# An mLSTM mixer's value product and output gate with features on partitions, and its head norm by products with ones

## The chip, the cores and the metric

One Trainium2 chip, one of its cores. The metric is the device time of one execution in microseconds (us). The kernel's weights, 292 MB with everything that is moved, come from the chip's memory in each execution.

## The reference

A trunk of two layers over 256 context tokens and 256 latent tokens of 1024 features. Layer 0 is a bidirectional chunkwise mLSTM mixer with 4 heads, layer 1 multi-head latent attention; behind each stands a gated convolutional feed-forward network. The change touches the mixer of layer 0. Cut to what it touches:

```python
x_m = h @ w_up                                   # 1024 -> 2048
x_c = silu(dwconv(x_m))
q, k = split(x_c @ w_qk)                         # 4 heads of 256
v = x_m @ w_v                                    # 4 heads of 512
s = chunk_scan(q, k, v, gates)                   # both directions, summed; per head: weights @ v
o = sigmoid(h @ w_og)                            # 1024 -> 2048, 4 heads of 512
hsum = o * s
y = head_rms_norm(hsum, norm_g) @ w_out          # per token and head over 512 features, eps 1e-6
```

The output is the latent stream in fp32.

## The kernel before

**Products.** Every operand is fp32 and is split in two: `hi`, a rounded copy (made by ACT), and `lo`, the rest (made by DVE, source minus `hi`). One product is three matmuls, hi x hi, hi x lo, lo x hi (`mm3`, lines 464 to 466). A tile is 128 partitions by 512 columns; sums lie in eight PSUM banks of that size.

**Weights.** `Stream` brings the weights in chunks of 128 x 1024 fp32 (512 KB) in a fixed order, `_plan`; `_stat` lays a chunk out as stationary operand (eight blocks of 128 x 128), `_mov` as moving operand (two rows of 512). SP issues the loads to `raw`, ACT casts `w` hi (lines 367 and 377), DVE subtracts `w` lo (lines 368 and 380). There are three `w` buffers, so that the cast of chunk n+3 waits until the products of chunk n have ended.

**Order.** Each engine works through its own queue in order. That order is fixed when the kernel is built: a scheduler places the instructions of all stages by its own estimate of readiness, not always as the code is written. A stage's main products are interleaved with background generators: `tick`, called once per weight chunk, advances the first generator in `bg` by one step, and the second begins when the first has ended. `drain` runs them to their end.

**The mixer's stages** (function `build`):

1. `w_up`: 16 chunks of `w_up`; with the convolution, `x_c` and sums of `x_m` go to memory.
2. `w_og`, 109 to 197 us: 16 chunks `og`, four for each head `s`. `tokmm` holds four banks, one per group `t` of 128 tokens: stationary is `hT` (tokens become partitions), moving the weights. After four chunks `evac` makes four sigmoids `o` and writes them to `od` in memory on ACT's queue (lines 883 and 884).
3. `w_v`, from 197 us: the value product, by a scheme with fewer multiplications over sums `s` of `xs`; chunks `vt2` and on, 12 matmuls each, and `vt2` chunks are also written back (`t2d`).
4. For h = 0 to 3: `w_qk(h)`, eight chunks of 24 matmuls, with `gate_chain`, `post(h - 2)` and `head(h - 1)` as background; then `av(h - 1)`, then `s_mm(h)`, the scores.
   - `head` makes the weights `W` (tokens by tokens), normalises them, and transposes the needed 128 x 128 blocks by PE into `PT[0..2]`, each split in hi and lo.
   - `v_load` and `v_steps` bring `v` and `od` back by POOL's queue (`vr`, `oh`).
   - `av` multiplies: per token group `t` stationary `PT` blocks, moving `v` of 512 features; context tokens need two blocks, latent tokens four. DVE multiplies the bank by the gate into `oh`.
   - `post` is the head norm over the 512 features, which lie along the free axis: ACT squares with a running sum into `ss` (128 x 1 each), square root, reciprocal 128 x 4 on DVE, four multiplications by a scalar per partition; later 16 transposes `hnT` on PE, and from their banks the split `hn` (hi on ACT at line 1248, lo on DVE at line 1249, both with the norm's weight `mng` as a scalar per partition). `hn[k]`, k = 4h + e, has features on partitions.
5. The output product "mout", context tokens first: 16 chunks of 12 matmuls of 512 columns (`outmm`; chunk k needs `hn[k]`, stationary). Under chunks 0 to 7 run `head(3)` and `post(2)`; then `av(3)`; under 8 to 11 `post(3)`; then 12 to 15. Under them also runs the modulation of the later stages (`junk<-ar,bc` on DVE). Then 16 chunks for the latent tokens, with the layer norm of the context tokens as background.

## Time and profile before

| | |
|---|---|
| three runs | 1343.89, 1345.22, 1345.07 us; median 1345.07 |
| the profiled execution | 1345.53 us, of which the span 1343.8 |
| granted clock of the PE array | 0.999 |
| PE, DVE, ACT, POOL busy | 99%, 80%, 53%, 9% of the span |
| matmul records | 6671 |
| memory read and written | 260.28 MB and 30.58 MB |

PE is TensorE's array, PEld its weight loads (they overlap), DVE VectorE, ACT ScalarE, POOL GpSimd, SP SyncE. A row of the timeline reads: start in us, length in us, engine, line, operation, output<-inputs, shapes, count, and in brackets how long the engine sat idle before it and what ended the wait. A row of the groups reads: line, engine, operation, output<-inputs, count | busy us, mean ns of one | idle us ahead of it and what ended most of it. The queue of an engine is written with a q (ACTq, POOLq, SPq): these rows are DMA issues.

### The profile page before, as it was taken

What the parts mean: (1) busy time and instruction counts of PE and PEld (TensorE: products, weight loads), DVE (VectorE), ACT (ScalarE), POOL (GpSimd) and SP (SyncE); (2) the same over time, 40 slices, a digit from 0 to 9 for tenths busy, and PEclk for the clock granted to TensorE, in tenths of its full rate; (3) what the DMA queues carried; (4) which work ended last, traced back from release to release, by engine and by line L of the source; (5) the groups of instructions that cost most, each with busy time, mean ns of one, the idle gap of its engine ahead of it and who ended that gap; (6) DMA issues with size and microseconds to landing.
All of it is one profiled execution on the core that took longest, in us unless ns stands there. A gap on an engine that the chain in (4) does not pass through costs nothing.

```text
span 1343.8 us, 18757 instructions
## 1 busy us (share of the span) xinstructions
PE 1333.9 (99%) x6671; PEld 1121.2 (83%) x6671; DVE 1072.5 (80%) x1774; ACT 708.1 (53%) x1240; POOL 123.1 (9%) x216
## 2 busy tenths in 40 slices
PE   9999999999999999999999999999999999999997
PEld 6877888888888888888898888888888988988886
DVE  5798766687888697787889878778787898898884
ACT  4675443445644545374643334333468767677661
POOL 0122000011011010210002000001100011000100
PEclk9999999999999999999999999999999999999999
DMA  9889748789765374666737777675877424476760
GB/s 375 298 292 342 227 172 256 233 281 309 251 212 196 110 240 133 224 215 211 245 107 257 235 241 238 225 245 165 233 264 244 127 82 162 150 219 194 266 188 32
DMA packets 88093, 292.09 MB, mean 217 GB/s; under 512 B 11640, under 2 KB 12152, under 8 KB 88000
## 3 DMA queue, kind: packets, MB, share of 16 engines
q1 hardware_dynamic: 61696, 215.75, 48.7%
q0 software_dynamic: 17520, 57.70, 13.8%
q10 hardware_dynamic: 8784, 17.45, 3.5%
q8 instruction: 52, 0.85, 0.3%
q14 instruction: 41, 0.34, 0.1%
HBM read 260.28 MB, written 30.58 MB: 216 GB/s over the span
## 4 chain that ended last, share of the span: by engine, by line
PE 95%; DMA 2%; DVE 1%; ACT 1%; issue 0%; DVEq 0%; ACTq 0%
PE fin L1602 8%; PE tok L464 6%; PE fin L465 6%; PE fin L466 6%; PE fin L464 6%; PE tok L466 6%; PE tok L465 6%; PE y L1686 5%; PE qk L466 4%; PE qk L464 4%; PE qk L465 4%; PE y L465 4%; PE y L466 4%; PE y L464 4%; PE up L747 2%; PE up L464 1%
## 5 line engine op out<-in xcount | busy, mean ns | idle before, releaser
L380 DVE TENSOR_TENSOR w<-raw,w 128x1024 fp32r<-128x1024 f32 (+1 forms) x256 | 307.7, 1205 | 112.0 <-ACT w L377 110.9
L377 ACT CAST w<-raw 128x1024 fp32r<-128x1024 f32 (+1 forms) x256 | 265.3, 1038 | 240.6 <-PE tok L466 83.7
L601 DVE SCALAR_TENSOR_TENSOR junk<-ar,bc 128x1024 f32<-128x1024 f32 x128 | 155.8, 1217 | 4.4 <-ACT mod L616 2.7
L465 PE MATMUL fin<-h,w 128*128 128x512 f32 (+1 forms) x376 | 141.2, 376 | 0.0
L464 PE MATMUL fin<-h,w 128*128 128x512 f32 (+1 forms) x376 | 141.2, 376 | 0.0
L466 PE MATMUL fin<-h,w 128*128 128x512 f32 (+1 forms) x376 | 141.1, 375 | 0.0
L1602 PE MATMUL fin<-h,w 128*128 128x256 f32 (+1 forms) x624 | 108.7, 337 | 0.0
L1602 PEld LDWEIGHTS fin<-h,w 128*128 128x128 f32 x624 | 95.9, 190 | 12.5
L464 PE MATMUL qk<-xc,w 128*128 128x512 f32 x256 | 100.4, 392 | 0.0
L466 PE MATMUL qk<-xc,w 128*128 128x512 f32 x256 | 99.7, 390 | 0.0
L465 PE MATMUL qk<-xc,w 128*128 128x512 f32 x256 | 99.6, 389 | 0.0
L465 PEld LDWEIGHTS fin<-h,w 128*128 128x128 f32 x376 | 70.8, 188 | 13.0
L464 PEld LDWEIGHTS fin<-h,w 128*128 128x128 f32 x376 | 70.7, 188 | 13.0
L466 PEld LDWEIGHTS fin<-h,w 128*128 128x128 f32 x376 | 70.8, 188 | 12.6
L466 PEld LDWEIGHTS qk<-xc,w 128*128 128x128 f32 x256 | 48.0, 188 | 10.1
L465 PEld LDWEIGHTS qk<-xc,w 128*128 128x128 f32 x256 | 48.1, 188 | 9.8
L464 PEld LDWEIGHTS qk<-xc,w 128*128 128x128 f32 x256 | 48.1, 188 | 9.7
L784 ACT ACTIVATE fg<-fg 128x512 f32<-128x512 f32 (+1 forms) x44 | 23.1, 526 | 57.0 <-DVE fg L782 50.8
L464 PE MATMUL tok<-w,hT 128*128 128x512 f32 x128 | 49.9, 390 | 0.0
L466 PE MATMUL tok<-w,hT 128*128 128x512 f32 x128 | 49.8, 389 | 0.0
L465 PE MATMUL tok<-w,hT 128*128 128x512 f32 x128 | 49.8, 389 | 0.0
L1686 PE MATMUL y<-w,fz 128*128 128x512 f32 x198 | 47.2, 394 | 0.3 <-DVE w L380 0.2
(492 smaller groups left out, 3138.4 us busy)
## 6 DMA issues: line engine op xcount, KB each, us to landing
raw<-in_ws SPq DMA_DIRECT2D x281, 512.0 KB, 4.7
ar<-in_adaT SPq DMA_DIRECT2D x80, 512.0 KB, 4.8
raw<-in_ws POOLq DMA_DIRECT2D x13, 512.0 KB, 7.2
raw<-in_ws SPq DMA_DIRECT2D x12, 384.0 KB, 6.2
adaw<-in_adaf SPq DMA_DIRECT2D x8, 512.0 KB, 6.2
xmd<-xr POOLq DMA_DIRECT2D x16, 256.0 KB, 4.7
xcd<-cv POOLq DMA_DIRECT2D x16, 256.0 KB, 4.8
xs<-xmd POOLq DMA_DIRECT2D x16, 256.0 KB, 5.6
```

The lines of the kernel that those rows point to most:

```text
L377: k.nc.scalar.copy(h[:, :cols], src)
L380: k.nc.vector.tensor_sub(l[:, :cols], src, h[:, :cols])
L464: mm(out, w[0], x[0], start=start, stop=False)
L465: mm(out, w[0], x[1], start=False, stop=False)
L466: mm(out, w[1], x[0], start=False, stop=stop)
L601: nc.vector.scalar_tensor_tensor(o, w, 1.0, self.bc[j], op0=ALU.mult, op1=ALU.mult, accum_out=col[:, k, j:j + 1])
L747: nc.tensor.matmul(ps[m], w[f][:, wi, m * 128:(m + 1) * 128], self.hT[f][:, hi], start=done[0] == 1, stop=done[0] == 24)
L784: nc.scalar.activation(tmp[:, :n], tmp[:, :n], AF.Silu)
L1602: nc.tensor.matmul(ps[:, :m], w[x][:, k * 128:(k + 1) * 128], hT(k)[:, :m], start=k == 0 and x == j, stop=k == 7 and x != j, skip_group_ch ...
L1686: nc.tensor.matmul(ps[b], a[:, p, ts], w[q][:, cs], start=j == 0 and n == 0 and not more, stop=j == end and n == 2, skip_group_check=True)
```

## The change

- The output gate is made with weights stationary and `hT` moving: each of the 16 chunks gives one bank of 128 features by 512 tokens, and each bank has its sigmoid and its write at once. The chunks' number and size and the number of matmuls stay.
- `head` groups the transposed blocks by the source block: `PT[0]` and `PT[1]` hold all four token groups of source 0 and 1, `PT[2]` those of sources 2 and 3 for the two latent groups.
- `av` has `v` stationary and `PT` moving. For each group `e` of 128 features: six matmuls of 512 tokens and six of the 256 latent tokens. Its result has features on partitions, so that nothing has to be transposed.
- `post` sums over partitions: ACT squares the four `oh`, DVE adds them, the sum is split, and two products with a matrix of ones (`ones`, 128 x 128) leave the sum over all 512 features in each partition of a bank `rms`. Then a square root and a reciprocal over the whole 128 x 512, and per `e` one operation (`oh` times `mng` times `rms`) and a split into `hn`. One `yield` more stands between the products with ones and the rest.
- Head 3 is normed in two halves: `av(3)` multiplies by the gate for tokens 0 to 255 and 256 to 511 apart; `post` of the first half is background of output chunks 8 to 11, of the second half of chunks 12 to 15, and each is drained behind them.

Counts: PE loses 64 transposes, has 96 matmuls of 512 and 96 of 256 columns in `av` for 144 of 512, and gains six of 512 and four of 256 with ones. DVE loses four reciprocals of 128 x 4 and 16 multiplications by a scalar, and reads 16 times fewer from PSUM for `hn`; it gains additions, reciprocals of 128 x 512 (three) and 128 x 256 (two), and the products with `rms`. POOL and SP keep their number of instructions.

```diff
@@ _plan, _pack
-    for s in range(4):
-        for c in range(4):
-            add(("og", s, c), 1024)
+    for m in range(16):
+        add(("og", m, 0), 1024)
...
-            b = _mov(i["m_w_og"][0][:, a * 512:(a + 1) * 512], 2 * c, 2)
+            b = _stat(i["m_w_og"][0], a, 0, 8)
@@ w_og
+        for m in range(16):
+            w = st.use(("og", m, 0))
+            ps = self.ps("tok")
+            for k in range(8):
+                c = slice(k * 128, (k + 1) * 128)
+                self.mm3(ps, (w[0][:, c], w[1][:, c]), (self.hT[k][:, 0], self.hT[k][:, 1]), k == 0, k == 7)
             self.tick(1, ADA_T)
+            if m == 1:
+                self.gates()
             o = self.s2("o")
+            nc.scalar.activation(o, ps, AF.Sigmoid)
+            nc.scalar.dma_start(self.od[m // 4, m % 4], o)
@@ head
+        for grp in ([(t, 0) for t in range(4)], [(t, 1) for t in range(4)], [(t, s) for s in (2, 3) for t in (2, 3)]):
@@ av
+        for e in range(4):
             ps = self.ps("av")
+            es = slice(e * 128, (e + 1) * 128)
+            for s in range(4):
+                x = PT[s] if s < 2 else PT[2][:, :, (s - 2) * 256:(s - 1) * 256]
+                o = ps if s < 2 else ps[:, 256:512]
+                for n, (i, j) in enumerate(((0, 0), (0, 1), (1, 0))):
+                    nc.tensor.matmul(o, v[s][:, i, es], x[:, j], start=s == 0 and n == 0, stop=s == 3 and n == 2,
+                                     skip_group_check=True)
@@ post
+        for e in range(4):
+            q = self.s2("sq")
+            nc.scalar.activation(q[:, c], tt[e][:, c], AF.Square)
+            if e:
+                nc.vector.tensor_tensor(sq[0][:, c], sq[0][:, c], q[:, c], op=ALU.add)
+            sq.append(q)
+        u = self.u("sq")
+        self.split(u[:, 0, c], u[:, 1, c], sq[0][:, c])
         yield
         if h < 2:
             yield
+        ps = self.ps("rms")
+        for x in range(2):
+            nc.tensor.matmul(ps[:, c], self.ones, u[:, x, c], start=x == 0, stop=x == 1)
+        r = self.s2("rms")
+        nc.scalar.activation(r[:, c], ps[:, c], AF.Sqrt, bias=self.keps, scale=1.0 / 512.0)
+        nc.vector.reciprocal(r[:, c], r[:, c])
+        yield
...
+            nc.vector.scalar_tensor_tensor(tt[e][:, c], tt[e][:, c], g[:, k:k + 1], r[:, c], op0=ALU.mult, op1=ALU.mult)
+            self.split(u[:, 0, c], u[:, 1, c], tt[e][:, c])
@@ build
-        tt = k.av(3)
-        k.bg = [k.post(3, tt)]
+        halves = slice(0, 256), slice(256, 512)
+        tt = k.av(3, halves)
+        k.bg = [k.post(3, tt, halves[0])]
         k.outmm("mout", range(8, 12), hn, pc, 0, 16, 1)
         k.drain()
+        k.bg = [k.post(3, tt, halves[1])]
...
         k.outmm("mout", range(12, 16), hn, pc, 0, 16, 1, n2=ADA_M)
+        k.drain()
```

**Where instructions stand.** ACT's queue at the end of the output gate, before. `L377 CAST w` with a `t2d` write behind it is the first value chunk, the two later casts of `w` the second and third; `o<-tok` are the last four sigmoids.

```order
L377 CAST w<-raw 128x1024
L379 DMA t2d<-raw 128x1024
L469 CAST s_1806<-xs_1636 128x512
L377 CAST w<-raw 128x1024
L469 CAST s_1811<-xs_1637 128x256
L469 CAST s_1811<-xs_1730 128x256
L883 ACTIVATE o<-tok 128x512
L884 DMA od<-o 128x512
L883 ACTIVATE o<-tok 128x512 x2
L884 DMA od<-o 128x512 x2
L883 ACTIVATE o<-tok 128x512
L377 CAST w<-raw 128x1024
```

The same place in the changed kernel; `L376 CAST w` with `t2d` behind it is the first value chunk, the sigmoid is that of the last gate chunk.

```order
L468 CAST s_1813<-xs_1643 128x512
L468 CAST s_1818<-xs_1644 128x256
L468 CAST s_1818<-xs_1729 128x256
L871 ACTIVATE o<-tok 128x512
L468 CAST s_1886<-xs_1728 128x512
L872 DMA od<-o 128x512
L376 CAST w<-raw 128x1024
L378 DMA t2d<-raw 128x1024
L376 CAST w<-raw 128x1024 x3
```

The cast of the first value chunk stood ahead of the last sigmoids and now stands behind the last one, a cast of `s` and the `od` write.

ACT's queue ahead of `av(3)`, before; the first `w` is output chunk 9, the last chunk 10.

```order
L1234 ACT_TABLE_LOAD
L1234 ACTIVATE ss<-ss,keps 128x4
L367 CAST w<-raw 128x1024
L469 CAST PT<-PT 128x512 x2
L469 CAST v<-vr 128x512
L1248 ACTIVATE hn<-hnT,sm 128x512 x4
L367 CAST w<-raw 128x1024
```

And in the changed kernel; the pair of `w` is chunks 8 and 9, the single one chunk 10.

```order
L366 CAST w<-raw 128x1024 x2
L468 CAST PT<-PT 128x512
L366 CAST w<-raw 128x1024
L468 CAST v<-vr 128x512
L468 CAST PT<-PT 128x512 x2
L468 CAST v<-vr 128x512
L468 CAST sq<-sq 128x512
L1234 ACT_TABLE_LOAD
L1234 ACTIVATE rms<-rms,keps 128x512
```

The casts of `PT`, `v` and now of the sum of squares moved behind the cast of chunk 10, and the square root behind them all.

PE's queue between output chunk 7 (`w_5184` with `hn[7]`, `hn_4568`) and `av(3)` in the changed kernel:

```order
L465 MATMUL y_4979<-w_5184,hn_4568 128x512
L1232 MATMUL rms_5199<-sq_5177,ones_79 128x512
L1205 MATMUL av_5259<-PT_5104,v_5027 128x512 x3
L1232 MATMUL rms_5199<-sq_5177,ones_79 128x512
L1205 MATMUL av_5259<-PT_5134,v_5079 128x512 x3
```

Head 2's products with ones stand behind chunk 7's last product, the second one within `av(3)`. The same queue between chunk 11 (`w_5352` with `hn[11]`, `hn_5235`) and chunk 12 (`w_5375` with `hn[12]`, `hn_5390`):

```order
L463 MATMUL y_4979<-w_5352,hn_5235 128x512
L464 MATMUL y_4979<-w_5352,hn_5235 128x512
L465 MATMUL y_4979<-w_5352,hn_5235 128x512
L1232 MATMUL rms_5367<-sq_5347,ones_79 128x256
L463 MATMUL y_4976<-w_5375,hn_5390 128x512
```

The second product with ones of head 3's first half stands between the two chunks.

Before, the last transposes of head 3 stand within and behind chunk 10 (`w_5291`); `w_5320` is chunk 11, and chunk 12 follows it with nothing between:

```order
L1245 MATMUL hnT_5335<-ident_68,oh_5225 128x128
L1245 MATMUL hnT_5343<-ident_68,oh_5225 128x128
L466 MATMUL y_4957<-w_5291,hn_5196 128x512
L1245 MATMUL hnT_5368<-ident_68,oh_5156 128x128 x2
L1245 MATMUL hnT_5368<-ident_68,oh_5225 128x128 x2
L1245 MATMUL hnT_5376<-ident_68,oh_5156 128x128 x2
L1245 MATMUL hnT_5376<-ident_68,oh_5225 128x128 x2
L464 MATMUL y_4954<-w_5320,hn_5204 128x512
```

The sum over head 3's features moved from ACT's running sums to PE, behind the last product of chunk 11, and what chunk 12 reads is made from it.

DVE's queue round the same place in the changed kernel; the first `w` is chunk 14's low half, `junk` the modulation.

```order
L602 SCALAR_TENSOR_TENSOR junk,mod_92<-ar,bc 128x1024
L367 TENSOR_TENSOR w<-raw,w 128x1024
L1235 RECIPROCAL rms<-rms 128x256
L1243 SCALAR_TENSOR_TENSOR oh<-oh,sm,rms 128x256 x3
L469 TENSOR_TENSOR hn<-oh,hn 128x256 x2
```

The reciprocal of the first half stands behind that low half.

More of the change, by code (lines that the diff above doesn't have):

```diff
@@ L519, in setup @@
         nc.vector.memset(self.zero.bitcast(F32), 0.0)
+        self.ones = p.tile([128, 128], F32R, name="ones")
+        nc.vector.memset(self.ones.bitcast(F32), 1.0)
         self.keps = p.tile([128, 1], F32, name="keps")
@@ L1226, in av, with post @@
         return r
-    def post(self, h, tt):
+    def post(self, h, tt, c=slice(0, 512)):
         nc = self.nc
-        ss = self.tiny(4, "ss")
-        jk = self.s2("jk")
-        for t in range(4):
-            nc.scalar.activation(jk, tt[t], AF.Square, accum_out=ss[:, t:t + 1])
-        nc.scalar.activation(ss, ss, AF.Sqrt, bias=self.keps, scale=1.0 / 512.0)
-        nc.vector.reciprocal(ss, ss)
-        for t in range(4):
-            nc.vector.tensor_scalar(tt[t], tt[t], ss[:, t:t + 1], None, op0=ALU.mult)
+        sq = []
+        for e in range(4):
+            q = self.s2("sq")
[5 more added lines that the diff above has]
+        self.split(u[:, 0, c], u[:, 1, c], sq[0][:, c])
         yield
@@ L1240, in post @@
             yield
+        ps = self.ps("rms")
[5 more added lines that the diff above has]
+        yield
         g = self.smc("mng")
         for e in range(4):
-            pt = self.ps("hnT")
-            for t in range(4):
-                nc.tensor.transpose(pt[:, t * 128:(t + 1) * 128], tt[t][:, e * 128:(e + 1) * 128], self.ident)
             k = h * 4 + e
-            u = self.u("hn")
-            nc.scalar.activation(u[:, 0], pt, AF.Copy, scale=g[:, k:k + 1])
-            nc.vector.scalar_tensor_tensor(u[:, 1], pt, g[:, k:k + 1], u[:, 0], op0=ALU.mult, op1=ALU.subtract)
-            self.hn[k] = u
+            if k not in self.hn:
+                self.hn[k] = self.u("hn")
+            u = self.hn[k]
+            nc.vector.scalar_tensor_tensor(tt[e][:, c], tt[e][:, c], g[:, k:k + 1], r[:, c], op0=ALU.mult, op1=ALU.mult)
+            self.split(u[:, 0, c], u[:, 1, c], tt[e][:, c])
             if e % 2:
```

44 lines of the change are left out of this document (6 added, 38 removed).

## The prediction

> **What bounds the kernel now.** I read the page's head and the chain of waits first, then the spacing of matmuls in the timeline, then the table of windows round the stages that the change touches.
>
> ```profile
> span 1343.8 us, 18757 instructions
> PE 1333.9 (99%) x6671; PEld 1121.2 (83%) x6671; DVE 1072.5 (80%) x1774; ACT 708.1 (53%) x1240; POOL 123.1 (9%) x216
> PE 95%; DMA 2%; DVE 1%; ACT 1%; issue 0%; DVEq 0%; ACTq 0%
> ```
>
> PE is busy for 99% of the span and carries 95% of the chain that ends last. "Busy" counts overlapping matmuls, so I check with start times. The 36 products of av(2), and the 12 products of 256 columns behind them:
>
> ```profile
> 502.91 0.39 PE L464 MATMUL av<-v,PT 128*128 128x512 f32 x1
> 510.84 0.39 PE L466 MATMUL av<-v,PT 128*128 128x512 f32 x1
> 511.07 0.28 PE L464 MATMUL sc<-qk 128*128 128x256 f32 x1
> 512.38 0.28 PE L466 MATMUL sc<-qk 128*128 128x256 f32 x1
> ```
>
> (510.84 - 502.91) / 35 = 0.227 us from start to start at 512 columns, (512.38 - 511.07) / 11 = 0.119 at 256. The products follow each other without a gap, so time can be won only by fewer or shorter products, and everything that makes PE wait is added in full. DVE is the engine with least slack. In the table of windows (length; PE, PEld, DVE, ACT, POOL busy; granted clock; DMA share, GB/s) the stretch ahead of av(2), and one behind head 3's norm:
>
> ```profile
> 456.00:502.00 46.00, 46.00 (x218) 38.40 (x217) 38.41 (x81) 26.91 (x59) 5.34 (x10) 1.00 0.55 178
> 631.00:642.00 11.00, 11.00 (x51) 9.06 (x50) 10.98 (x18) 5.59 (x9) 0.00 (x0) 1.00 0.76 263
> ```
>
> DVE has 7.6 of 46 us left per head there, and nothing left at 631 to 642.
>
> **PE's own work.** A head's 16 transposes stand in one run before the next qk product:
>
> ```profile
> 467.11 1.91 PE L1245 MATMUL hnT<-ident,oh 128*128 128x128 f32 x16
> 468.78 0.48 PE L464 MATMUL qk<-xc,w 128*128 128x512 f32 x1
> ```
>
> (468.78 - 467.11) / 16 = 0.104 each; 64 removed: -6.7 us. The value product goes from 144 of 512 columns to 96 of 512 and 96 of 256: 96 x 0.227 + 96 x 0.119 - 144 x 0.227 = +0.5. The products with ones, six of 512 and four of 256, add 6 x 0.227 + 4 x 0.119 = +1.8. The output gate keeps its 384 products of 512, and `PT` its 12 transposes per head. Sum: **-4.4 us**. ACT loses 16 squares with their reads of the accumulator and 16 evictions of hnT, and gets 20 squares, 5 casts of the sum and 20 casts of hn, many of 256 columns; at 53% busy I cost its amount at nothing, its order not. POOL and SP keep their instructions; POOL reads `od` first at head 1, two stages behind, which hides the writes in their new order.
>
> **Wait 1, gate to value.** Before, the last gate chunk and the first value chunk:
>
> ```profile
> 190.26 1.05 ACT L377 CAST w<-raw 128x1024 fp32r<-128x1024 f32 x1 [0.29 <-DVE raw L340]
> 197.09 0.39 PE L466 MATMUL tok<-w,hT 128*128 128x512 f32 x1
> 197.32 0.39 PE L464 MATMUL tok<-w,s 128*128 128x512 f32 x1
> 198.08 0.60 ACT L883 ACTIVATE o<-tok 128x512 f32<-128x512 f32 x1 [0.51 <-ACT o L883]
> 198.71 0.33 ACTq L884 DMA_DIRECT2D od<-o  x1
> 199.51 0.62 ACT L469 CAST s<-xs 128x512 fp32r<-128x512 f32 x1
> L368 DVE TENSOR_TENSOR w<-raw,w 128x1024 fp32r<-128x1024 f32 x28 | 34.1, 1217 | 12.6 <-ACT w L367 12.6
> 1336.28 0.28 PE L466 MATMUL y<-wg,act 128*128 128x256 f32 x1
> 1336.60 0.42 DVE L1284 TENSOR_TENSOR z<-z,y 128x256 f32<-128x256 f32 x1 [0.31 <-PE y L466]
> ```
>
> The first value chunk was cast at 190.26, seven us ahead of the last gate product at 197.09. After the change that cast stands on ACT behind the last sigmoid, which waits for the gate's last product, behind one cast of `s`, and behind the issue of the `od` write. Queued behind it are all value chunks' casts. Chain from the end of the product's slot: 0.2 until a reader starts (1336.28 + 0.12 to 1336.60), sigmoid and `s` cast in a row about 1.1, an issue that may or may not overlap 0 to 0.33, cast 1.05: PE stands still for 2.35 to 2.7. Two products with the high half take 0.45; the third needs DVE's low half, 1.22 behind the cast, so 0.8 more. Bounds 2.4 (low half hidden after all) and 4.2 (a late second chunk as well); I take **3.5**, the chain as it stands.
>
> **Wait 2, the norm on DVE (heads 0 to 2).** Rows for the prices:
>
> ```profile
> L1235 DVE RECIPROCAL ss<-ss 128x4 f32<-128x4 f32 x4 | 0.7, 177 | 15.2 <-ACT ss L1234 15.2
> L1810 DVE RECIPROCAL zs<-zs 128x1 f32<-128x1 f32 x4 | 0.4, 149 | 0.0
> L2032 DVE RECIPROCAL sm<-sm 128x1 f32<-128x1 f32 x16 | 2.6, 162 | 2.7 <-ACT P L2031 2.6
> 595.70 1.68 DVE L1237 TENSOR_SCALAR oh<-oh,ss 128x512 f32<-128x512 f32 x4
> 597.29 1.28 DVE L470 TENSOR_TENSOR PT<-PT 128x512 fp32r<-128x512 f32 x2
> 600.22 2.72 DVE L1249 SCALAR_TENSOR_TENSOR hn<-hnT,sm,hn 128x512 fp32r<-128x512 f32 x4
> L1611 DVE TENSOR_TENSOR fb<-fin,fb 128x256 f32<-128x256 f32 x44 | 17.8, 419 | 2.5 <-ACT fb L1610 2.5
> L1610 ACT COPY fb<-fin 128x256 f32<-128x256 f32 x44 | 15.9, 369 | 21.2 <-PE fin L1602 18.3 <-PE fin L1534 2.9
> ```
>
> No reciprocal of 512 elements per partition is in the trace. The widest has 4: (177 - 149) / 3 = 9.3 ns per further element against the one row, (177 - 162) / 3 = 5 against the other. At 512 the one gives 4.9 us, the other 2.7; the lower bound is an elementwise operation, 1.28 / 2 = 0.64. I take the middle of the two slopes, 7.2 ns: **3.8 us** at 512 and 2.0 at 256, since the only rows of the operation itself say that it grows faster than an addition. The Trainium skill ("VectorE: DVE Perf Modes", section "First, the fixed hardware budget") says that a reciprocal is an iterative divide with a repeat count of 8; read as 8 cycles per element at the 0.96 GHz of the same page's "Specifications" that is an estimate of 4.3 us at 512, and the sum would rise by about 1 us; the slopes of the trace lie on its side, an addition's price does not.
>
> Per head DVE gets 3 additions, a split of the sum, 4 products and 4 low halves, 12 x 0.64 = 7.7, and 3.8; it loses 4 x 0.42 + 4 x 0.68 + 0.18 = 4.6. Net +6.9, so 38.4 becomes 45.3 of 46. In those windows queued behind the reciprocal are the low half of a qk chunk, the normalising of the scores and the splits of `PT` and `v`, for which av waits. There is cover left, but nearly none. I take +1 for head 2's stretch, +0.7 for head 3's; bounds 0 (a reciprocal of 0.64) and 3 each.
>
> **Wait 3, ahead of av(3).** In the new order PE runs head 2's two products with ones directly behind the last product of output chunk 7, ahead of av(3). Their operand is cast on ACT at the end of a row that begins with the cast of chunk 10, which waits until chunk 7 frees its buffer.
>
> ```profile
> 596.29 1.06 ACT L469 CAST PT<-PT 128x512 fp32r<-128x512 f32 x2
> 597.25 0.63 ACT L469 CAST v<-vr 128x512 fp32r<-128x512 f32 x1
> L1234 ACT ACT_TABLE_LOAD x3 | 3.8, 1283 | 0.1
> L1234 ACT ACTIVATE ss<-ss,keps 128x4 f32<-128x4 f32 x4 | 1.2, 296 | 0.0
> ```
>
> 0.2 + chunk cast 1.05 + `v` 0.55 + two `PT` 1.06 + `v` 0.55 + sum 0.55 = 3.95. The second product needs the low half from DVE, behind chunk 10's low half and four splits; three av products (0.7) run meanwhile, and about 0.6 is left. I take **4.5**; bounds 3.5 (casts overlap by 0.1 each) and 5.2. Before, the same casts of `PT` and `v` were made while PE ran the hnT transposes. Behind that comes the norm itself: table load 1.28, square root, 3.8, product, cast, split, some 7.5 us for hn[8], against 24 products of 512 and 24 of 256 of av, 8.3 us: +0.7, bounds 0 and 1.5.
>
> **Wait 4, ahead of chunk 12.** Head 3's first half (tokens 0 to 255) has its second product with ones behind chunk 11's last product, and chunk 12's first product next. Between them: 0.2, the cast of chunk 14 on ACT 1.05 (it waits for chunk 11's buffer), DVE's low half of it 1.22, which stands ahead of the reciprocal, 2.0, product 0.42, cast 0.37: **5.2 us** in which PE does nothing; bounds 3.6 (reciprocal 0.42) and 6. Before, the last transposes stood ahead of chunk 11, which covered the eviction, and nothing stood between chunks 11 and 12. The second half's chain runs under chunk 12 to 15 and is needed only by the latent tokens; cover 12 x 0.227 = 2.7 us per chunk.
>
> **Wait 5.** At 631 to 642 DVE is full already, and the second half's 2.0, splits and products come on top: the layer norm's rows come later by a part of it. +0.8, bounds 0 and 3.
>
> **Sum.** 3.5 + 1.7 + 4.5 + 0.7 + 5.2 + 0.8 = 16.4; less 4.4: +12.0. It is made against the profiled execution, 1345.53 us (span 1343.8 and 1.7 around it), 0.46 above the median of the three runs. 1345.53 + 12.0 - 0.46 = 1357.1, rounded to **1357**.
>
> **The rivals.**
>
> *The reciprocal is cheap.* At 0.64 and 0.42 wait 4 falls by 1.6, wait 2 by 1.4, hn[8] and wait 5 by 1.2: 1357.1 - 4.2 = 1352.9. Against it: two slopes. For it: they rest on 15 to 28 ns.
>
> *The waits cost clock too.* At the end of the kernel PE stands still, and the table of windows shows the granted clock:
>
> ```profile
> 1339.00:1340.00 1.00, 0.00 (x0) 0.00 (x0) 1.00 (x3) 0.00 (x0) 0.00 (x0) 1.00 0.00 0
> 1340.00:1341.00 1.00, 0.00 (x0) 0.00 (x0) 0.59 (x1) 0.00 (x0) 0.00 (x0) 0.76 0.20 76
> 1341.00:1342.00 1.00, 0.00 (x0) 0.00 (x0) 0.00 (x0) 0.00 (x0) 0.00 (x0) 0.50 1.00 373
> 1.49 3.35 PE L721 MATMUL up<-zero 128*128 128x512 f32 x7 [1.49 <-DVE zero L519]
> 5.11 1.00 PE L552 MATMUL adar<-adaw,condp 128*32 128x256 f32 x8 [0.27 <-DVE condp L536]
> ```
>
> The last product ends at 1336.28 + 0.28 = 1336.56; the clock falls to 0.5 at about 1340.5, 4 us later. Coming from rest, the first seven products took 3.35 / 7 = 0.48 each, twice the slot, and from 5.11 on eight of 256 take 0.125 each, full speed: some 3.5 us at half speed, so 1.8 us lost per trip. Wait 4 (5.2) is long enough, wait 3 (4 in one piece) at the edge, wait 1 not: 1357.1 + 1.8 = 1358.9 with one trip, 1360.7 with two. The Trainium skill ("TensorE: Matmul & The Clock Gate", section "What's actually happening") says the same as a rule: half clock after an idle window of about 3.4 us that runs freely, full clock after a busy one; by it wait 4 may or may not contain a whole window, and wait 3 seldom. The 4 us above fit it.
>
> *DVE becomes the bound.* If the reciprocal is at 4.9 us, head 2's and head 3's stretches need 46.4 of 46 us and wait 2 goes to 3 + 3, hn[8] to 1.5, wait 5 to 2: 1364.
>
> *The other side: the waits are hidden, only PE's work counts.* The mechanism is ACT running ahead at one place after the other: it loses 32 operations, and if each cast were done before the product that frees PE, the new time would be 1345.07 - 4.4 = 1340.7. It decides only if all waits together stay under 1.7 us. The cast of chunk 10 and the last sigmoid start by a release that PE itself gives, so waits 1, 3 and 4 can't be entered early; I see no room for it but an order that I misread.
>
> **How the numbers follow.** Forecast as it stands 0.45; clock as well 0.23; cheap reciprocal 0.14; DVE as bound 0.08; hidden waits 0.05; and 0.05 for waits of half the size, which ends at about 1345.07 - 4.4 + 8.2 = 1349. Range 1350 to 1362: the lower bounds of all waits give 1345.07 - 4.4 + 2.4 + 3.5 + 3.6 = 1350.2, the upper end takes in both trips of the clock and leaves out the DVE-bound case; what is left out is some 0.18. A measurement of this kernel can tell about 0.2%, 2.7 us, from no change. Faster by more: 0.05. Within: half the waits at their smallest, 0.05. Slower: 0.90.
>
> **What would show it.** Wait 1: a cast of the first value chunk right behind a sigmoid, and 2 to 3 us between two `tok` products. Wait 3: the first `rms` product about 4 us behind the last product of chunk 7, released by ACT. Wait 4: 5 us between chunks 11 and 12, with a reciprocal of about 2 us in it. The reciprocal's row: 3.8 us; under 1 or over 4.8 would move the sum as above. A granted clock under 1 behind waits 3 or 4 would show that rival. I am wrong if PE still runs without gaps at these three places, or if DVE's lag before av(1) and av(2) is the larger part.

## The result, and the profile after

The changed kernel takes 1367.06 us (median of 1365.06 to 1369.03), the kernel before 1344.57 in the same comparison: ratio 1.0164, 95% interval 1.0153 to 1.0175, so 22 us slower. The profiled execution is 1367.06 with a span of 1365.3, against 1345.53 and 1343.8 before.

The head of the page and its chain of waits, after:

```profile
span 1365.3 us, 18750 instructions
PE 1341.0 (98%) x6665; PEld 1123.7 (82%) x6665; DVE 1098.5 (80%) x1808; ACT 711.1 (52%) x1238; POOL 123.1 (9%) x216
PE 95%; DMA 2%; ACT 1%; DVE 1%; issue 0%; DVEq 0%; SPq 0%; ACTq 0%
```

PE has less work to do and is busy for 7 us longer: its matmuls themselves took longer. Where the time went shows when the first product of each stage is looked up in the two timelines:

| stretch, from first product to first product | before | after | difference |
|---|---|---|---|
| start to the output gate | 109.05 | 109.30 | +0.25 |
| gate to value product | 88.27 | 91.77 | +3.50 |
| value product to scores of head 0 | 197.37 | 200.85 | +3.48 |
| scores of head 0 to scores of head 3 | 175.43 | 174.05 | -1.38 |
| scores of head 3 to output chunk 0 | 4.18 | 4.19 | +0.01 |
| output chunk 0 to output chunk 12 | 46.23 | 55.12 | +8.89 |
| output chunk 12 to the first product of the feed-forward | 56.30 | 64.24 | +7.94 |
| from there to the last product | 659.45 | 658.29 | -1.16 |

The heads' own stretch became shorter, as its removed transposes would have it. Everything else lies at four places. The three that were forecast, in the timeline of PE after:

```profile
197.34 0.39 PE L465 MATMUL tok<-hT,w 128*128 128x512 f32 x1
201.07 0.79 PE L463 MATMUL tok<-w,s 128*128 128x512 f32 x1 [3.35 <-ACT w L376]
603.19 0.39 PE L465 MATMUL y<-w,hn 128*128 128x512 f32 x1
607.24 0.79 PE L1232 MATMUL rms<-sq,ones 128*128 128x512 f32 x1 [3.66 <-ACT sq L468]
630.10 0.31 PE L1232 MATMUL rms<-sq,ones 128*128 128x256 f32 x1
635.28 0.80 PE L463 MATMUL y<-w,hn 128*128 128x512 f32 x1 [4.87 <-ACT hn L468]
```

Between the slots the waits are 201.07 - 197.34 - 0.23 = 3.5, 607.24 - 603.19 - 0.23 = 3.8 and 635.28 - 630.10 - 0.12 = 5.1 us. Behind each wait a product lasts 0.79 or 0.80, not 0.39. The table of windows shows why (columns as in the prediction's; the granted clock is the third number from the end):

```profile
200.00:201.00 1.00, 0.00 (x0) 0.00 (x0) 1.00 (x2) 1.00 (x2) 0.00 (x0) 0.56 0.22 86
206.00:207.00 1.00, 1.00 (x3) 0.74 (x3) 1.00 (x2) 0.00 (x0) 0.00 (x0) 0.53 0.02 8
606.00:607.00 1.00, 0.00 (x0) 0.00 (x0) 1.00 (x2) 1.00 (x3) 0.00 (x0) 0.65 0.68 242
613.00:614.00 1.00, 1.00 (x6) 0.83 (x5) 1.00 (x1) 0.24 (x1) 0.00 (x0) 0.93 0.00 0
633.00:634.00 1.00, 0.00 (x0) 0.00 (x0) 1.00 (x1) 0.00 (x0) 0.00 (x0) 0.81 1.31 246
640.00:641.00 1.00, 1.00 (x5) 0.78 (x5) 0.00 (x0) 0.29 (x1) 0.00 (x0) 0.78 1.11 303
```

At each wait the clock falls to half (from 0.56 = x + 0.5 (1 - x), x = 0.12, at 200.1; in the same way at 606.3 and 633.6) and comes back only 5.2 to 5.9 us after the products have begun again (from 0.53 = 0.5 x + (1 - x), x = 0.94, at 206.9; then at 613.1 and 640.4). Summed over windows of 1 us, PE's busy time by what the clock lacked is 2.8, 3.0 and 2.6 us. The fourth place is behind them, in the last latent chunks:

```profile
684.81:688.22 3.41, 1.82 (x6) 0.97 (x6) 2.14 (x3) 2.95 (x4) 0.00 (x0) 1.00 0.14 56
688.00:689.00 1.00, 1.00 (x4) 0.40 (x3) 1.00 (x2) 1.00 (x2) 0.00 (x0) 0.61 0.00 0
691.00:692.00 1.00, 1.00 (x4) 0.78 (x3) 0.65 (x3) 0.00 (x0) 0.00 (x0) 0.68 1.01 377
```

There PE waits four times for a wide weight chunk, 2.8 us in all, and the clock halves there too, from 688.2 to 691.6 (1.7 us). In the list of waits ACT stands for the load of these chunks, and SP's queue, which issues the loads in order, for DVE's low half that frees the buffer:

```profile
ACT wu L366 <- DMA raw<-in_ws: 4.8, 2, 3.4
SPq L327 <- DVE wu L367: 12.5, 3, 7.7
```

The account: waits 3.5 + 0.7 (third product of the first value chunk) + 3.8 + 5.1 + 2.8 = 15.9, half clock 2.8 + 3.0 + 2.6 + 1.7 = 10.1, PE's own work -4.4: 21.6, where the table's differences add up to 21.5. The sum leaves out small waits, such as 0.6 in the heads (below), so its agreement to 0.1 is in part chance.

The times of the clock show a pattern. It was at half for 6.8, 6.8, 6.8 and 3.4 us, and the full stretches between them, 399.4, 20.5 and 47.8 us, are 117, 6 and 14 times 3.413: all eight changes lie on one grid of 3.41 us. So they do in each of the 15 traces (the kernel before, the changed one, and the 13 edits below), each with a grid that begins elsewhere. What goes with a fall is how long PE was busy in the 3.41 us ahead of a grid point: 1.02, 0.69, 0.20 and 1.82 us ahead of these four falls (the row from 684.81 shows the last). Over all 15 traces, at full clock, less than 46% always led to a fall, more than 62% never did, and between them both occurred. So where a wait lies on the grid decides with its length whether the clock falls, and whether the half clock then lasts 3.4 or 6.8 us.

### The profile page after: what moved, and what is told of

Read it like the earlier page. It is cut to its first block, busy times and chain, and to the rows that moved or that the text cites. A ratio compares the mean times of both kernels' runs of the same rounds, so it can differ in the third digit from the quotient of the medians.

```text
span 1365.3 us, 18750 instructions
## 1 busy us (share of the span) xinstructions
PE 1341.0 (98%) x6665; PEld 1123.7 (82%) x6665; DVE 1098.5 (80%) x1808; ACT 711.1 (52%) x1238; POOL 123.1 (9%) x216
## 4 chain that ended last, share of the span: by engine, by line
PE 95%; DMA 2%; ACT 1%; DVE 1%; issue 0%; DVEq 0%; SPq 0%; ACTq 0%
PE fin L1596 8%; PE y L1680 7%; PE fin L464 6%; PE fin L465 6%; PE tok L464 6%; PE fin L463 6%; PE tok L465 6%; PE tok L463 6%; PE qk L465 4%; PE qk L463 4%; PE qk L464 4%; PE y L464 4%; PE y L463 4%; PE y L465 4%; PE av L1205 3%; PE up L748 2%
## 5 line engine op out<-in xcount | busy, mean ns | idle before, releaser
L376 ACT CAST w<-raw 128x1024 fp32r<-128x1024 f32 (+1 forms) x256 | 265.0, 1038 | 239.2 <-PE tok L465 72.2
L465 PEld LDWEIGHTS qk<-xc,w 128*128 128x128 f32 x256 | 48.0, 188 | 10.1
L463 PE MATMUL tok<-hT,w 128*128 128x512 f32 x128 | 49.9, 390 | 0.0
L465 PE MATMUL tok<-hT,w 128*128 128x512 f32 x128 | 49.8, 389 | 0.0
L464 PE MATMUL tok<-hT,w 128*128 128x512 f32 x128 | 49.8, 389 | 0.0
L463 PE MATMUL y<-w,hn 128*128 128x512 f32 x108 | 43.7, 405 | 4.9 <-ACT hn L468 4.9
```

The costliest lines, as they stand in the source:

```text
L376: k.nc.scalar.copy(h[:, :cols], src)
L463: mm(out, w[0], x[0], start=start, stop=False)
L464: mm(out, w[0], x[1], start=False, stop=False)
L465: mm(out, w[1], x[0], start=False, stop=stop)
```

## The experiments

Theory after the trace: (1) three waits and late weight chunks, each with a cause of its own; (2) every wait costs some 2.5 to 3 us more by the clock; (3) nothing else. The rivals stand with each run. Edits are to the changed kernel, where no other is named. Times "above" are against the kernel before in the same comparison.

**The gate's end: whose wait is it?** The trace agrees with the forecast's cause in part only. ACT's and DVE's rows there:

```profile
198.26 0.61 ACT L468 CAST s<-xs 128x512 fp32r<-128x512 f32 x1
199.97 1.04 ACT L376 CAST w<-raw 128x1024 fp32r<-128x1024 f32 x1 [1.11 <-DVE raw L339]
198.72 1.22 DVE L339 TENSOR_TENSOR raw<-raw 128x1024 f32<-128x1024 f32 x1
195.02 2.05 DVE L469 TENSOR_TENSOR s<-xs,s 128x512 fp32r<-128x512 f32 x4 [10.78 <-ACT s L468]
```

The first value chunk's cast was held up twice. It stands behind the last sigmoid and a cast of `s`, which ended at 198.87 (198.26 + 0.61); with that alone, an estimate from these rows, PE would have waited about 2.4 us. Then it waited 1.1 us more for DVE's sum of weights (198.72 + 1.22 = 199.94). That sum stood behind low halves of `s`, for which DVE had sat idle for 10.8 us, and ACT's list of waits has the casts of `s` waiting for PE's `tok` products. These casts write into buffers that `hT` held. Before, a group of four chunks ran through the feature blocks of `hT` in order, so that its last readers of `hT[0]` and `hT[1]` came with chunk 12; with weights stationary every chunk reads all of `hT`, and all of it is held until chunk 15.

```diff
-        for m in range(16):
+        for ms in [(m,) for m in range(14)] + [(14, 15)]:     # last two chunks block by block together
...
+            for k in range(8):
+                for w, ps in zip(ws, pss):
+                    self.mm3(ps, (w[0][:, c], w[1][:, c]), (self.hT[k][:, 0], self.hT[k][:, 1]), k == 0, k == 7)
```

> The last two gate chunks are multiplied together, feature block k by feature block k, so that the last reader of hT[0] comes about 10 us ahead of the gate's end and not 5 us. The first value chunk stands behind the gate's end by 3.5 us in the changed kernel, and the granted clock halves there for 6 us, some 7 us in all. Theory A (buffers: ACT's casts of s wait for the buffers of hT, DVE's low halves of s wait for these casts, the sums of value weights wait on DVE's queue behind them, and the cast of the first value chunk waits for the sums): the wait falls under 1 us, the clock stays full, the kernel is 6 to 8 us faster than the changed one, about 1360. Theory B (queue, as predicted: the cast only stands behind the last sigmoid on ACT): the wait stays 2.4 to 3.6 us and the time is the same within 1 us, 1366 to 1368.

Measured: 1361.91 us, ratio 1.0119 (1.0101 to 1.0137), 5 us less than the changed kernel's median; the profiled spans differ by 6.8 (1358.5). ACT's rows show the casts set free block by block, and PE goes on without the wait:

```profile
190.75 0.62 ACT L468 CAST s<-xs 128x512 fp32r<-128x512 f32 x1 [3.48 <-PE tok L465]
192.11 0.71 ACT L468 CAST s<-xs 128x256 fp32r<-128x256 f32 x2 [0.74 <-PE tok L465]
196.21 1.05 ACT L376 CAST w<-raw 128x1024 fp32r<-128x1024 f32 x1 [0.76 <-DVE raw L339]
197.47 1.07 ACT L875 ACTIVATE o<-tok 128x512 f32<-128x512 f32 x2
197.35 0.70 PE L463 MATMUL tok<-w,s 128*128 128x512 f32 x2
```

The casts begin 1.36 us apart, the time of six products. By its time that is about theory A, and the buffers are shown: the casts of `s` and DVE's sums come earlier. But the edit moved two things. The sigmoids stand at the same time as before it (197.47 against 197.76), while the chunk's cast now stands ahead of them in ACT's queue. So the run doesn't separate the buffers from the order; the rows of the changed kernel do: the order was worth about 2.4 us of the wait of 3.5, the buffers the last 1.1. Some 1.2 us of wait for the chunk's low half is left. 1.7 us of the difference between the spans are the half clock behind the weight chunks: waits of about the same length there lay otherwise on the grid, and the clock held.

**What is the clock's share?**

```diff
+    def fill(self, n, ps=None):                      # products of ones with ones, read by nobody
...
+        self.fill(FILL[0])                           # behind the gate; also ahead of head 2's ones, and of chunk 12
```

> Adds matmuls of ones with ones, 128 columns, whose result nobody reads: 28 behind the last gate product, 28 ahead of head 2's products with ones, 42 between output chunks 11 and 12, at about 0.1 us each. They lie in the three waits of PE and end before these do. Theory A (the halved clock is a cost of its own, beside the waits): the granted clock stays 1.00 behind the three places, the waits keep their lengths of 3.5, 3.8 and 5.1 us (counted from the last real product to the next), the kernel is 7 to 9 us faster than the changed one, 1358 to 1360. Theory B (the clock costs nothing because what follows waits for DVE and ACT anyway): no faster than 1365.

Measured: 1367.39 us, ratio 1.0156 (1.0133 to 1.0179): no gain in the median; the profiled execution is the fastest of four, 1363.24. But the fillers did not do what they should at two of three places. Behind the gate they ended at 200.8, and:

```profile
201.00:202.00 1.00, 0.49 (x1) 0.19 (x1) 1.00 (x3) 1.00 (x2) 0.00 (x0) 1.00 1.00 406
202.00:203.00 1.00, 0.44 (x2) 0.40 (x3) 1.00 (x2) 0.88 (x1) 0.00 (x0) 0.97 0.04 12
```

Two us at half occupation, with no wait over 1.3 us, were enough to halve the clock: in the 3.41 us ahead of the fall at 202.9 PE was busy for 2.11 (62%), fillers included. So once more, with fillers that reach to the third product:

```diff
-FILL = 28, 28, 42
+FILL = 46, 46, 42
```

> As e2_fill, whose fill matmuls took 0.116 us each and ended 0.4 to 2.2 us ahead of the next real products, with the clock halved behind two of the three places all the same. Now 46, 46 and 42: 5.3, 5.3 and 4.9 us, so that PE is busy until the operands of the third product are there too. Theory A (the half clock is a cost of its own: about 2.7 us at each of the three places in the changed kernel's profile, for waits that stay as long): clock 1.00 at all three, 5 to 8 us faster than the changed kernel, which stands 22.5 above the kernel before: 14.5 to 17.5 above. Theory B (behind the waits DVE and ACT set the pace, and a full clock only brings new waits): 20 or more above.

Measured: 1364.54 us, ratio 1.0137 (1.012 to 1.0154), 18 above: between the theories. The clock now stays at 1.00 at all three places:

```profile
205.00:206.00 1.00, 1.00 (x8) 0.87 (x8) 1.00 (x4) 0.47 (x1) 0.00 (x0) 1.00 0.00 0
610.00:611.00 1.00, 1.00 (x4) 0.85 (x5) 0.00 (x0) 0.47 (x1) 0.54 (x1) 1.00 0.35 143
```

From value product to scores the stretch is 3.1 us shorter than in the changed kernel, from chunk 12 to the feed-forward 1.4. But the gate's stretch is 1.6 longer (the fillers overran), and at the late weight chunks the waits and the half clock remain. So of the 8.4 us that the three halvings cost in the changed kernel's trace, a kernel that keeps its waits gets back 3 to 4 by the ratios, whose intervals just touch: the half clock is a cost of its own, and the rest comes back as overrun and as waits for DVE further on.

One more thing stands in this trace. The gate begins at 111.85 us, in the changed kernel's at 109.30, though nothing was changed ahead of it. Six of the first `up` products, in the trace of e11, which has the same late start, and in that of the kernel before:

```profile
10.99 2.76 PE L748 MATMUL up<-hT,w 128*128 128x512 f32 x6
9.16 1.66 PE L747 MATMUL up<-hT,w 128*128 128x512 f32 x6
```

In five of the 15 traces (e5, e7, e8, e9, e11) the clock became full only at 13.4 to 14.5 us, in the others at 4.4 to 7.6; the gate began at 111.5 to 112.0 in the five, at 109.0 to 109.3 in the others. These are traces of different kernels, but what differs lies ahead of all that was edited; so it seems that executions of one kernel can differ by 2.2 to 3.0 us in this way too. With four to six executions per kernel, a difference of 2 to 3 us between two edits is not safe.

**The reciprocal.** Its row and that of the halves:

```profile
L1235 DVE RECIPROCAL rms<-rms 128x512 f32<-128x512 f32 x3 | 10.0, 3348 | 1.6 <-ACT rms L1234 1.6
632.52 1.75 DVE L1235 RECIPROCAL rms<-rms 128x256 f32<-128x256 f32 x1
```

```diff
-        nc.vector.reciprocal(r[:, c], r[:, c])
+        nc.vector.tensor_scalar(r[:, c], r[:, c], 1.0, None, op0=ALU.mult)
```

This kernel leaves out the inverse and multiplies by the root itself; it serves to price the operation.

> The five wide reciprocals are replaced by a multiplication by 1.0 of the same shape (the norm's factor is then the root itself, not its inverse). Theory A: DVE gets 3 x 2.7 + 2 x 1.35 = 10.8 us back, but only the ones on a waited-for chain count: the wait ahead of output chunk 12 falls from 5.1 to about 3.7 us, and the late weight chunks at 684 us come earlier by some 1.4 us; the half-clock stretches stay. 2 to 4 us faster than the changed kernel, about 1364. Theory B (DVE's load by the reciprocal is the main cause of the loss): 8 us or more faster, under 1359.

Measured: 1355.74 us, ratio 1.0079 (1.0058 to 1.0101), 11 us less than the changed kernel. Theory A was too small, because it left out the clock: the wait ahead of chunk 12 falls to 1.9 and no longer halves the clock (5.1 - 1.9 + 2.6 = 5.8), and the late weight chunks are gone with their half clock (2.8 + 1.7 = 4.5). The waits of 3.5 and 3.8 stay; behind the second the half clock lasted 3.4 us instead of 6.8, which is another 1.5; the wait is the same, so that part is the grid's, not the edit's. Then with an operation that gives the same norm without DVE:

```diff
-        nc.scalar.activation(r[:, c], ps[:, c], AF.Sqrt, bias=self.keps, scale=1.0 / 512.0)
-        nc.vector.reciprocal(r[:, c], r[:, c])
+        nc.scalar.activation(r[:, c], ps[:, c], AF.Abs_reciprocal_sqrt, bias=self.keps, scale=1.0 / 512.0)
```

> Square root and wide reciprocal become one ACT operation (the inverse root), everything else as changed. Leaving the reciprocals out (a multiplication in their place) gave 1355.7. Theory A (the reciprocal's place in DVE's queue makes the wait ahead of chunk 12 and the late weight chunks): the same or a little better than that, 1353 to 1356; the wait ahead of av(3) stays 3.8 us and that behind the gate 3.5, both with a halved clock behind. Theory B (the multiplication's saving came from somewhere else, such as the root's range): over 1360.

Measured: 1357.19 us, ratio 1.0073 (1.0058 to 1.0088); the kernel before stood at 1346.81 in this comparison, so 10 above against 11 in the run before. What PE still waited for, from its list of waits:

```profile
PE rms L1232 <- ACT sq L468: 3.7, 1, 3.7
PE tok L463 <- ACT w L376: 3.3, 1, 3.3
PE tok L464 <- DVE w L379: 0.8, 1, 0.8
```

Chunk 12's operand has gone from the list, and the wide weight chunks too. That the two runs differ by less than 1 us shows no more than that they are alike.

**The late weight chunks: DVE's load or the loads' order?**

```diff
-        k.outmm("mout", range(12, 16), hn, pc, 0, 16, 1, n2=ADA_M)
+        k.outmm("mout", range(12, 16), hn, pc, 0, 16, 1)
...
-        k.outmm("mout", range(6), hn, pl, 256, 16, 1, n2=ADA_M)
+        k.outmm("mout", range(6), hn, pl, 256, 16, 1)
```

> The modulation steps (a DVE operation of 1.22 us each) are left out of output chunks 12 to 15 and of the latent chunks 0 to 5 and are done later, in the next stage; some 6 operations, 7.3 us of DVE. In the changed kernel PE waits for the low halves of the last wide weight chunks at 684 to 688 us, with a halved clock behind, 5 us in all against the kernel before. Theory A (DVE is late there, so the raw buffers come free late and SP issues their loads late): that wait goes, 4 to 5 us faster than the changed kernel, about 1362, unless the modulation makes the next stage late. Theory B (the loads are late for another reason, such as SP's queue standing behind the half clock's delay): same time, 1366 to 1368.

Measured: 1367.69 us, ratio 1.0163 (1.0141 to 1.0186), no change in sum, but not theory B. The waits at 684 us are gone, and the moved operations made one elsewhere:

```profile
951.11 1.22 PE L1680 MATMUL y<-w,fs 128*128 128x512 f32 x2 [3.91 <-DVE w L379]
```

4.1 us and 2.7 us of half clock there. So the weight chunks were late by DVE's load, and the wait moves with the load.

**The halves.**

```diff
-        tt = k.av(3, halves)
-        k.bg = [k.post(3, tt, halves[0])]
+        tt = k.av(3)
+        k.bg = [k.post(3, tt)]
...
-        k.bg = [k.post(3, tt, halves[1])]
```

> Undoes the halves alone: head 3's norm is made in one piece ahead of chunk 12, otherwise as changed. Theory A (the reciprocal's length is on the path ahead of chunk 12, and the second half's DVE work is what makes the last weight chunks late): the wait ahead of chunk 12 becomes 6 to 7.5 us (3.35 for 1.75 us of reciprocal), its half clock stays, and the waits at 684 us with their half clock (5 us) shrink to under 2: 1364 to 1367, about the same as the changed kernel. Theory B (the halves save nothing at the end, the last weight chunks are late for another reason): 1369 or more.

Measured: 1366.9 us, ratio 1.0147 (1.013 to 1.0163): as theory A, a zero sum. Ahead of chunk 12:

```profile
633.07 0.51 PE L1232 MATMUL rms<-sq,ones 128*128 128x512 f32 x1 [1.66 <-ACT sq L468]
634.63 0.57 PE L1232 MATMUL rms<-sq,ones 128*128 128x512 f32 x1 [1.05 <-DVE sq L469]
640.80 0.80 PE L463 MATMUL y<-w,hn 128*128 128x512 f32 x1 [5.60 <-ACT hn L468]
```

Some 9 us of wait in three pieces against 5.1, more than either theory had, and none at the weight chunks.

**The wait ahead of av(3).** ACT's queue there, in the changed kernel:

```profile
603.62 1.04 ACT L366 CAST w<-raw 128x1024 fp32r<-128x1024 f32 x1 [1.46 <-PE y L465]
606.56 0.63 ACT L468 CAST sq<-sq 128x512 fp32r<-128x512 f32 x1
```

The first cast waits until chunk 7 has ended, and behind it stand two casts of `v`, two of `PT` and, last, that of the sum, for which PE waits. Moving that one cast behind them:

```diff
+        if key == ("mout", 0, 10) and 10 not in self.once:
+            self.once.append(10)
+            with k.tc.issue_after(k.sqi.ins):            # the cast of the sum of squares
+                k.nc.scalar.copy(h[:, :cols], src)
```

> One instruction of the changed kernel is queued elsewhere: ACT's cast of output chunk 10, which waits until chunk 7 ends, stands behind the casts of v, PT and the sum of squares, not ahead of them. In the changed kernel's trace ACT waits 1.5 us at its place with these casts ready behind it. Theory A (the wait ahead of av(3) is this queue: five casts stand behind one that waits for PE): the casts run under chunk 7, the wait falls from 3.8 to 0 to 1.5 us and the half clock behind it goes; ahead of chunk 12 the wait stays about 5 us: 4 to 7 us faster than the changed kernel, 15.5 to 18.5 above the kernel before. Theory B (the casts' operands themselves come late, from DVE): under 2 us faster, 20.5 or more above.

Measured: 1365.73 us, ratio 1.0151 (1.0137 to 1.0166). The place did what theory A says, the time did not:

```profile
603.19 0.64 ACT L1232 CAST sq<-sq 128x512 fp32r<-128x512 f32 x1
603.88 0.50 PE L1239 MATMUL rms<-sq,ones 128*128 128x512 f32 x1 [1.15 <-ACT sq L1232]
```

3.8 us became 1.3, and the clock stays at 1.00 there; but ahead of chunk 12 the waits grew from 5.1 to 6.3 in three pieces, and those for the weight chunks from 2.8 to 3.7. The profiled span came down by 4.2, the median by under 2; the profiled execution is the fastest of four. What is won at one place is in part lost at the next; that DVE's lag is why is likely, but was not tried out here.

**Several together.** The inverse root on ACT with the two gate chunks:

> The run with the inverse root on ACT and the last two gate chunks together. If the losses add up place by place (theory A), the 5 to 7 us of the gate's end come off as well: 1347 to 1350, with one wait of 3.8 us and one half-clock stretch left ahead of and behind av(3). Theory B (the places share slack, a gain at one is lost at the next): 1352 or more.

Measured: 1352.11 us, ratio 1.0033 (1.002 to 1.0046), 4.4 above by that ratio. The time itself lies at theory B's edge, but the kernel before stood 2 us higher in this comparison; against the run with the inverse root alone it is 5 us less, as theory A, with 3.8 us ahead of av(3), 0.7 in it and 1.5 by half clock left. Two tries to put PE work there, with head 2's norm ahead of head 3's weights, or with three background steps per chunk:

```diff
-        k.bg = [k.head(3, S, True), k.post(2, tt)]
+        k.bg = [k.post(2, tt), k.head(3, S, True)]
...
-            k.outmm("mout", range(i, i + 1), hn, pc, 0, 16, 2)
+            k.outmm("mout", range(i, i + 1), hn, pc, 0, 16, 3)
```

> As the run before, but head 2's norm is background ahead of head 3's weights in output chunks 0 to 7 (three steps per chunk), so that its products with ones stand in chunks 1 and 2 and one to two chunks of PE work stand between the transposes of PT and av(3). Theory A (the wait ahead of av(3) is the row of casts behind chunk 10's, with nothing for PE to do; with work in between it is hidden): that wait and its half clock go, 3.8 + 2.9 = 6.7 us; but head 3's norm then has only 1 to 2 chunks of cover ahead of chunk 12, and 0 to 4 us come back there. 1341 to 1347, and at the low end faster than the kernel before. Theory B (PE's gain of 4 us is eaten by DVE whatever the order): 1348 or more.

> e6_ars_pair with one number changed: three background steps per output chunk 0 to 7, not two. The transposes of head 3's PT then stand in chunk 6, and the whole of chunk 7 (2.7 us) stands between them and av(3). e6 stood 4.4 us above the kernel before, with 3.8 us of wait ahead of av(3), 0.7 in it, 1.5 by the half clock. Theory A (that wait is the casts of PT, v and the sum behind chunk 10's weight cast, and PE has nothing else): the wait falls to 0.5 to 2 us, the clock stays full: 0 to 2 above the kernel before, at the low end equal to it. Theory B (DVE can't have PT ready a chunk earlier, so PE waits for the transposes' operands in chunk 6 by as much): 4 or more above.

Measured: 1352.63 (ratio 1.0041, 1.0026 to 1.0056) with both lines, 1351.55 (1.0043, 1.0031 to 1.0055) with the second alone. Both missed theory A and lie where theory B has them. PE's waits with both lines, in the list:

```profile
PE y L464 <- DVE w L367: 3.3, 2, 2.6
PE PT L1156 <- DVE W L1145: 2.0, 2, 1.7
PE y L463 <- ACT hn L468: 1.4, 1, 1.4
```

With both lines DVE cannot normalise `W` and make low halves a chunk earlier; PE waits for it instead, up to 2.6 us at a time, and the clock never falls ahead of the last product. So theory (2) doesn't hold for every wait: this one of 2.6 us is split by a grid point, and PE is busy for 58% and 67% of the two steps. With the second line alone theory B's wait for the transposes does not show: 2.3 us are left ahead of av(3), and 3.5 in three pieces came up ahead of chunk 12, with half clock behind both. And with the additions of the squares on POOL:

```diff
-                nc.vector.tensor_tensor(sq[0][:, c], sq[0][:, c], q[:, c], op=ALU.add)
+                nc.gpsimd.tensor_tensor(sq[0][:, c], sq[0][:, c], q[:, c], op=ALU.add)
```

> e10 with the three additions of the squares per norm on POOL, not on DVE (POOL adds 128 x 512 in about 1.4 us where DVE takes 0.6). DVE gets 3 x 0.6 us back per head in stretches where it is full, the chain to the products with ones gets 3 x 0.8 us longer. Theory A (DVE's load bounds the stretch ahead of av(3)): 1 to 3 us faster than e10. Theory B (the length of the chain to the products with ones counts, above all ahead of chunk 12): 1 to 4 us slower than e10, with a wait at the first half's products.

Measured: 1356.37 us, ratio 1.0073 (1.0059 to 1.0088), slower than e10 by 4, as theory B has it. But the longer chain is not the whole cause. Of the 5.3 us between the profiled spans 2.5 lie ahead of the gate. In its list PE's wait for the cast of the sum of squares is 2.7 us, as in e10; the longest entry is 2.9 us, for the transposes of `PT`. Ahead of them, POOL and DVE in this run, and the same two rows of DVE in e10:

```profile
590.49 5.69 POOL L1227 TENSOR_TENSOR sq<-sq 128x512 f32<-128x512 f32 x3 [29.33 <-ACT sq L1225]
591.10 1.63 DVE L1145 SCALAR_TENSOR_TENSOR W<-W,R,W 128x384 f32<-128x384 f32 x1
592.66 1.24 DVE L1134 SCALAR_TENSOR_TENSOR R<-den 128x2 f32<-128x2 f32 x1
588.57 0.61 DVE L1145 SCALAR_TENSOR_TENSOR W<-W,R,W 128x384 f32<-128x384 f32 x1
589.10 0.15 DVE L1134 SCALAR_TENSOR_TENSOR R<-den 128x2 f32<-128x2 f32 x1
```

While POOL adds, these DVE operations take 1.0 and 1.1 us longer, and a third at 594.95 as well. Neither theory had that; how much of the 4 us is the chain and how much this stays open.

Last, the inverse root, the two gate chunks and the moved cast together:

> The last two gate chunks together, the inverse root on ACT, and the cast of chunk 10 queued later. e6 without the last stood 4.4 us above the kernel before and had 3.8 + 0.7 us of wait and 1.5 of half clock round av(3). Theory A (the losses were these three places and nothing else; what is left is PE's own work, 4.4 us less than before, and 1 to 2 us of small waits): 1 to 3 us faster than the kernel before. Theory B (the added work of ACT and DVE costs something at other places whatever the order): 2 us or more above it.

Measured: 1349.39 us, ratio 1.0034 (1.0021 to 1.0047). That is theory B's side. In the profiled execution (1347.47, 1.9 above that of before) the clock stays full from 4.4 us to the last product, and PE waits for

```profile
PE rms L1243 <- ACT sq L1236: 1.2, 1, 1.2
PE tok L470 <- DVE w L385: 1.1, 1, 1.1
PE y L470 <- DVE wu L373: 1.0, 3, 0.7
```

and 0.4 for `hn`. Those are 3.7 us of waits against 4.4 us less work, which would leave it 0.7 below the kernel before; the other 2.6 us are not in the list. Its stretches show where they lie: from the value product to the scores of head 0 it is 1.45 longer than the kernel before, from output chunk 12 to the feed-forward 2.87, while the heads are only 1.15 shorter and the stretch of output chunks 0 to 12 only 0.31. It does not beat the kernel before, and theory A's "nothing else" is not shown. The executions of this kernel spread from 1346.68 to 1351.97; the clock's start, 2.2 to 3.0 us, may be half of that spread, but one trace can't show it. Of the 22 us, some 18 are accounted for by edits.

## Why the prediction was wrong

**The direction and the waits were right, and their sum by luck nearly exact**: 16.4 forecast, 16.5 in the trace with the 0.6 in the heads. Waits 1 and 5 were forecast too low and the others too high, by nearly as much. Term by term:

- PE's own work, -4.4: the heads' stretch holds two norms and three av, for which the forecast's prices give 2 x (0.45 - 16 x 0.104) + 3 x 0.14 = -2.0; measured -1.4, so 0.6 of wait there against 1.7 forecast. DVE had cover enough in the heads.
- Wait 1, 3.5 with the low half: measured 3.5 and 0.7, with half the mechanism. The forecast read the order and saw the cast behind the sigmoid; that chain, 2.35 to 2.7 by its prices, is there with 2.4. The other 1.1 it did not have: the cast then waited for DVE, DVE for ACT's casts of `s`, these for buffers. Which buffers a moved loop holds until when was not asked, and the order doesn't show it.
- Wait 3, 4.5: measured 3.8, mechanism as forecast (e12).
- Wait 4, 5.2: measured 5.1, with 1.75 for the reciprocal where 2.0 was taken; hn[8] came in time.
- The reciprocal: 3.35 us at 512, 6.3 ns per further element ((3348 - 1745) / 256), inside the two slopes 5 and 9.3. The Trainium skill ("VectorE: DVE Perf Modes", section "First, the fixed hardware budget"), read as eight cycles per element, gave an estimate of 4.3; at the 0.96 GHz of that page the measured 6.3 ns are 6 cycles, and the measurement decides.
- Wait 5, +0.8 with an upper bound of 3: the term that was mis-sized among the waits. It measured 2.8, and not at the rows of the layer norm, but at the weight chunks behind them: DVE's low halves free the raw buffers, SP's queue issues the loads in order, and a load takes its 4.6 us. e4, e5 and e8 take it away, e3 moves it.

**The step that failed is the clock.** The sum left it out; the rival put it at "wait 4 is long enough, wait 3 at the edge, wait 1 not", 1.8 us per trip and at most two trips, with a chance of 0.23. Measured: four trips, 10.1 us; without them the forecast's sum stands at 1357, with them at 1367. Both of its numbers came from too few events. The threshold of 4 us was read at the kernel's end from one event; here the clock fell 2.4 us after the last product (197.34 + 0.39 to 200.1), 2.7 and 3.2, and e2 shows it fall without any wait over 1.3. The grid of 3.41 us says why one event could not give it: the time until the fall depends on where the last product lies on the grid, and the 4 us at the end were 0.5 to the next grid point and 3.4 without any work. And 1.8 per trip was read at the start of the kernel, where 3.5 us at half speed were seen; that is the price of one step of the grid, as the fourth trip shows (1.7). Behind the three waits the half clock lasted two steps, and cost 2.6 to 3.0.

The Trainium skill ("TensorE: Matmul & The Clock Gate", section "HAM oscillation — how this bites in real kernels") gives as a rule that PE should have no idle gap over about 3.4 us, and describes a kernel that falls to half clock again at each such gap. The direction agrees with these traces. The limit doesn't: the clock fell after 2.4 and 2.7 us without a product, and after a stretch in which PE was 53% busy (684.8 to 688.2), and the measurements decide.

What the rivals said: the cheap reciprocal was no reciprocal of this chip, but e4 shows that its price was 11 us, not 4.2, since it decides about the clock at one place and the loads at another (and some 1.5 of the 11 are the grid's). DVE as the bound was right in one stretch (from the output chunks to the feed-forward) and wrong in the heads. The hidden waits did not occur.

## What to carry to other kernels

Where PE is the bound, a change that saves it work but puts a chain of other engines between two products pays twice: the wait, and the half clock behind it, here 1.5 to 3.2 us each time the clock fell in these stages. By the shares above, an estimate: a single gap over some 3.7 us (two times 54% of 3.41) always falls, one under 1.3 us (38% of 3.41) never, and between them the grid decides, which a kernel does not choose. Several short gaps within one step count together, as those of the weight chunks did. Price each new gap with both, and ask of every loop whose operands stay in use for longer which buffers that holds back and who is waiting for them. When the remedy moves work in time, follow the engine that is full (here DVE) to the next place: two of these edits, e3 and e12, gave back most of what they had won.

## What was not expected of the hardware

- The granted clock changes only on a grid of 3.41 us, in all 15 traces. At full clock it fell whenever PE was busy for less than 46% of a step, and never above 62%. In the changed kernel that was 2.4 to 3.2 us after PE's last product, and it was full again 5.2 to 5.9 us after products had begun; in other runs it took as little as 2.9 us (e4, 607.36 to 610.29). It held at 1.00 through 5 us bridged with products of 128 columns that nobody reads.
- While POOL adds tensors of 128x512, DVE operations that take 0.15 and 0.61 us otherwise (e10) took 1.24 and 1.63 (e11).
- DVE's reciprocal takes 3.35 us for 512 elements per partition and 1.75 for 256, five times an addition (0.68 alone).
- One inverse root on ACT takes 0.69 us at 512 columns and 0.47 at 256, as long as the square root that it replaces.
